# Attention logits with queries stacked as high over low part, and keys twice over each other

## The chip, the cores and the metric

The kernel runs on one core of one Trainium2 chip. The metric is the device time of one launch in microseconds. Engine names are short: PE is TensorE (matmul), ACT is ScalarE, DVE is VectorE, POOL is GpSimd, SP is SyncE, which here issues most DMA transfers. PSUM is the memory that PE writes its sums into, SBUF the one that holds everything else on the core.

## The reference

One decoder layer is computed on 256 tokens of 1024 features. The input is projected, three attention mixers share the projection, their outputs are gated, merged and normalised, and a feed-forward part follows:

```
proj = x @ w_in[i]
aq, ak, av, iq, ik, iw, bq, bk, bv, cq, ck, cv = jnp.split(proj, SPLIT_POINTS, axis=-1)
o_a = dsa_mixer(...)       # indexer scores pick 64 keys; 6 query heads on one shared key head
o_b = dilated_mixer(...)   # 3 groups x 4 query heads on 4 key heads
o_c = moba_mixer(...)      # 6 heads with a key head each
merged = sum of sigmoid(x @ w_gate) * (o @ w_br) over the three
x = layer_norm(ALPHA * x + merged @ w_out[i])
h = jnp.square(jax.nn.relu(x @ w_up[i])) @ w_down[i]
x = layer_norm(ALPHA * x + h + ple)
```

The part that matters here is the same in all mixers and in the indexer: for each head the logits, 64-long dot products of queries with keys,

```
logits = jnp.einsum('bqhd,bskd->bqhk', q, k) * HEAD_DIM ** -0.5     (then bias, mask, softmax)
```

There are 8 indexer heads, 12 dilated heads, 6 block heads and 6 sparse heads, 32 in all, over 256 queries in two blocks of 128.

## The kernel before, in words

All data is float32. PE multiplies in the faster float32r form, which keeps fewer bits, so every operand is split into a high part (the value cast to float32r) and a low part (what the cast lost). A product then takes three matmuls: high by high, high by low, low by high. `prod` (L127 to L129) does that for all large products. A split costs one ACT step, which casts, and one DVE step, which subtracts; for weights it is L70 (ACT) and L74 (DVE, and for part of the columns POOL).

The order of the work is as follows. The first four feature tiles (the indexer's queries) are projected with the arriving input (L402). Then one unit of weights after another is loaded by SP, split, and multiplied: `feat` projects 128 feature columns for all 256 tokens into one tile of the PSUM pool `mm`, and `fill` computes gates ("g") or merge products ("c") in between. `mm` has three tiles for all of these. Weights are split four units ahead. The code gives a priority by its order; a scheduler with a model of the time of each instruction draws up the order on each engine, and logits get a higher priority (L258).

A feature tile holds two heads of 64 features, head 0 on partitions 0 to 63 and head 1 on 64 to 127, as columns of tokens. `q_pair` (L204) splits such a tile of queries: one ACT step on all 128 partitions (L207) and one DVE step (L208). `k_pair` (L212) does it for keys (L218, L219). For the dilated and the block mixers it makes one ACT and one DVE step. For the two keys that all heads of a mixer share, `kI` (indexer) and `kA` (sparse mixer), it is called with the same 64 partitions twice and makes two of each, so that the key lies on both halves of the partitions.

`logits` (L254) takes a query tile and a key tile. For each of the two query blocks it makes six matmuls: low query by high key, high by high, high by low, each for head 1 and head 0. Each matmul uses 64 rows of the array, head 0 the upper and head 1 the lower, and `keep_in_program_order` (L267) keeps the two heads' matmuls side by side. The first query block needs 128 keys, the second 256. It is called 16 times: 4 for the indexer, 6 for the dilated mixer, 3 for the block mixer, 3 for the sparse one.

The logits then go through bias, softmax, transposes (L303 to L305) and the product with the values (L310 to L313); gates are read out of `mm` by ACT (L231), merge products by DVE (L244). After the mixers come the merge, the output projection, the normalisation and the feed-forward part.

Of the kernel before, what the change touches and what calls it, by code (L numbers as in the profile page):

```python
# [11 lines left out]
F32 = mybir.dt.float32  # L12
F32R = mybir.dt.float32r
ALU = mybir.AluOpType
# [6 lines left out]
S = 256  # L21
# [67 lines left out]
def hybrid_layer(ctx: ExitStack, tc: tile.TileContext, x0, xn, pT, wqk, wva, wvb, wg, wbc, wba,  # L89
                 wout, wup, wdn, wpg, wple, lnrow, rel, onehot, pick, out):  # L90
    nc = tc.nc
    pe, act, dve, pool = nc.tensor, nc.scalar, nc.vector, nc.gpsimd
# [48 lines left out]
    pm = mid.enter_context(tc.tile_pool(name="pm", bufs=1))  # L141
    one = ctx.enter_context(ExitStack())
    right = lambda n, b: one.enter_context(tc.tile_pool(name=n, bufs=b, side="right"))
    p1, k1, kp = (right(n, b) for n, b in (("p1", 1), ("k1", 2), ("kp", 3)))

    xh = p1.tile([128, KT, S], F32R, name="xh")
    xl = p1.tile([128, KT, S], F32R, name="xl")
# [12 lines left out]
    for t in TASKS:  # L160
# [4 lines left out]
        elif t in "gcao":  # L165
            u, w, n = {"g": (u_g, wg, 1024), "c": (u_bc, wbc, 640), "a": (u_ba, wba, 768),
                       "o": (u_out, wout, 1024)}[t]
# [28 lines left out]
    QC = (slice(0, 128), slice(128, 384))  # L196

    def mmbank(shape):
        t = mm.tile([128, 512], F32, name="mm", tag="mm")
        return t[:, 0:256] if shape == 256 else t  # L200

    last = [None]

    def q_pair(ps, scale=-0.125):  # L204

        q = qpool.tile([128, 2, S], F32R, name="q", tag="q")
        last[0] = act.mul(q[:, 0], ps, scale).ins  # L207
        dve.scalar_tensor_tensor(q[:, 1], ps, scale, q[:, 0].bitcast(F32), op0=ALU.mult,  # L208
                                 op1=ALU.subtract)
        return q  # L210

    def k_pair(a, b=None):  # L212


        k = (kp if b is None else k1).tile([128, 2, S], F32R, name="k", tag="k")
        for d, ps in ((slice(0, 128), a),) if b is None else ((slice(0, 64), a),
                                                             (slice(64, 128), b)):
            act.copy(k[d, 0], ps)  # L218
            dve.tensor_tensor(k[d, 1], ps, k[d, 0].bitcast(F32), op=ALU.subtract)  # L219
        return k  # L220

    n_g, n_c = [0], [0]

# [23 lines left out]
    def feat(f):  # L247
        ps = mmbank(256)
        gemm(ps, u_q[f], xs)
        if f > 4:  # L250
            next(side, None)
        return ps

    def logits(q, k):  # L254


        ss = [next(ps_s)[:, 0:384] for _ in range(2)]
        with tc.high_priority(offset=500):  # L258
            for b in range(2):
                c = slice(b * 128, (b + 1) * 128)  # L260
                for i, (x, y) in enumerate(((1, 0), (0, 0), (0, 1))):
                    for h in (1, 0):
                        d = slice(64 * h, 64 * h + 64)
                        m = pe.matmul(ss[h][:, QC[b]], lhsT=q[d, x, c],  # L264
                                      rhs=k[d, y, 0:128 * (b + 1)], start=i == 0, stop=i == 2)
                        if b or i or not h:
                            tc.keep_in_program_order(m)  # L267
        return ss

    V = p1.tile([128, 2, 11, 128], F32R, name="V")  # L270
# [71 lines left out]
    def slots(qs, k, Ts, vh, o):  # L342

        es = [wk2.tile([128, 3, 384], F32, name="eb", tag="eb") for _ in range(2)]
        mxs = [sm.tile([128, 2, 3], F32, name="mxb", tag="mxb") for _ in range(2)]
        for g in range(3):
            s = logits(qs[g], k)
            for h in range(2):
                for b, t in enumerate((Ts[h][:, g, 128:256], Ts[h][:, g, :])):
                    dve.tensor_tensor_reduce(es[h][:, g, QC[b]], s[h][:, QC[b]], t, op0=ALU.add,  # L350
                                             op1=ALU.min, scale=1.0, scalar=-GONE,
                                             accum_out=mxs[h][:, b, g:g + 1])
        for h in range(2):
            e = es[h]
            m = sm.tile([128, 2], F32, name="mx", tag="mx")
            den = sm.tile([128, 2], F32, name="den", tag="den")
            dve.tensor_reduce(m, mxs[h], axis=AX.X, op=ALU.min)
            for b in range(2):
                act.activation(e[:, :, QC[b]], e[:, :, QC[b]], AF.Exp, bias=m[:, b:b + 1],
                               scale=-1.0, accum_out=den[:, b:b + 1])  # L360
            pool.tensor_tensor(e[:, 0], e[:, 0], e[:, 1], op=ALU.add)
            pool.tensor_tensor(e[:, 0], e[:, 0], e[:, 2], op=ALU.add)
            scale_rows(e[:, 0], den)
            attend(e[:, 0], vh + h, o, h)
# [16 lines left out]
    with ExitStack() as begin:  # L381
        st = begin.enter_context(tc.tile_pool(name="st", bufs=1, side="right"))
        sh, sl = (st.tile([128, KT, FIRST * 128], F32R, name=n) for n in ("sh", "sl"))
        g0 = G.rearrange("p i s -> p (i s)").rearrange("p (k c) -> p k c", k=KT)
        cut = [((0, 384), (384, 768)) if k == 0 else ((0, 768),) for k in range(KT)]
        with tc.high_priority(offset=1000):
            for k in range(KT):
                for i, (a, b) in enumerate(cut[k]):
                    e = nc.scalar if i else nc.sync
                    e.dma_start(g0[:, k, a:b], x0[k, :, a:b])  # L390
            for k in range(KT):
                act.copy(xh[:, k], g0[:, k, 0:S])
                for a, b in cut[k]:
                    a = max(a, S)
                    act.copy(sh[:, k, a - S:b - S], g0[:, k, a:b])
                dve.tensor_tensor(xl[:, k], g0[:, k, 0:S], xh[:, k].bitcast(F32), op=ALU.subtract)
                dve.tensor_tensor(sl[:, k], g0[:, k, S:], sh[:, k].bitcast(F32), op=ALU.subtract)
        first = [next(ps_s if f < 3 else ps_t)[:, 0:S] for f in range(FIRST)]
        for k in range(KT):
            for i, (w, x) in enumerate(((sh, xh), (sh, xl), (sl, xh))):  # L400
                for f in range(FIRST):
                    pe.matmul(first[f], lhsT=w[:, k, 128 * f:128 * f + 128], rhs=x[:, k],  # L402
                              start=k == i == 0, stop=k == KT - 1 and i == 2)
        iq = [q_pair(ps, 0.125) for ps in first]
    tp, wk, wk2, sm = (right(n, b) for n, b in (("tp", 3), ("wk", 3), ("wk2", 2), ("sm", 6)))
    tab = bias_table()
    ps = feat(4)
    kI, kA = k_pair(ps[0:64], ps[0:64]), k_pair(ps[64:128], ps[64:128])

# [6 lines left out]
    for j in range(4):  # L418
        s = logits(iq[j], kI)
        r = wk2.tile([128, 768], F32, name="ri", tag="eb")  # L420
        r = r.rearrange("p (h k) -> p h k", h=2)
        for h in range(2):
            act.activation(r[:, h], s[h], AF.Relu)
            for b in range(2):
                n = 2 * j + h
                dve.scalar_tensor_tensor(idx[:, QC[b]], r[:, h, QC[b]], iw[:, b, n:n + 1],
                                         idx[:, QC[b]], op0=ALU.mult, op1=ALU.add)
# [16 lines left out]
    for j in range(2):  # L444
        ps = feat(5 + 4 * j)
        k = k_pair(ps)
        fill("g")
        qs = []
        for g in range(3):
            qs.append(q_pair(feat(6 + 4 * j + g)))  # L450
            if g:
                fill("g")
        o = opair()
        Ts = [toeplitz(6 + 2 * j + h, 4) for h in range(2)]
        slots(qs, k, Ts, 1 + 2 * j, o)
        pair_out(o, 3 + j)
        fill("g")
# [6 lines left out]
    for j in range(3):  # L464
        ps = feat(13 + 2 * j)
        k = k_pair(ps)
        q = q_pair(feat(14 + 2 * j))
        s = logits(q, k)
        o = opair()
        for h in range(2):  # L470
            n = 2 * j + h
            if n % 3 == 0:
                T = toeplitz(18 + n, 1)
            head(s, T[:, n % 3, 128:256], T[:, n % 3], 5 + n, o, h)
            fill("g")
        pair_out(o, 5 + j)
# [4 lines left out]
    for j in range(3):  # L481
        q = q_pair(feat(19 + j))
        s = logits(q, kA)
        o = opair()
        for h in range(2):
            n = 2 * j + h
# [144 lines left out]
    for b in range(2):  # L631
        t = slice(b * 128, (b + 1) * 128)
        for c in range(2):
            cs = slice(c * 512, (c + 1) * 512)
            ps = mmbank(512)
# [28 lines left out]
    for f in range(32):  # L664
        ps = mmbank(512).rearrange("p (b a t) -> p b a t", b=2, a=2)
# [4 lines left out]
        for k in range(KT):  # L670
            pe.matmul(ps[:, :, 0], lhsT=lo[:, cs[k]], rhs=x1[:, :, k, 0], start=False,  # L671
                      stop=k == KT - 1)
        r, q = (w2.tile([128, 2, 128], F32, name=n, tag=n) for n in ("r", "q2"))
# [3 lines left out]
        q = q.rearrange("p b t -> p (b t)")  # L677
# [126 lines left out]
```

## Time and profile before

| | |
|---|---|
| time, median of 3 runs | 452.64 us (451.95 to 453.76) |
| the profiled execution: time, span | 451.62 us, 449.8 us |
| instructions | 7880 |
| mean granted clock of TensorE | 0.996 |
| busy: PE, PE weight loads, DVE, ACT, POOL | 436.4, 396.1, 304.6, 260.9, 101.3 us |
| share of line 264 (logits) in the chain that ended last | 3.2% |

The span is the time from the first to the last instruction. The chain that ended last is followed back from the last instruction, at each step to what released it. Matmuls are pipelined: the time that a matmul lasts in a row is longer than the step from one to the next, so the start times of neighbours tell what one costs. In a row of the timeline the columns are the start (us), the duration (us), the engine, the line, the operation, output and inputs, the shape, and the number of instructions; the idle time before it and what ended it stand in brackets. In a group by line they are the output and inputs with shapes, the count, the busy us, the mean ns of one, and the idle us before with what ended it. In the waits they are the us in total, the times and the longest. In a stretch they are its bounds and length, and then the busy us and the count of PE, PEld (weight loads), DVE, ACT and POOL.

### The profile page before, as it was taken

How to read it: one execution, taken by the hardware profiler on the slowest of the kernel's cores; microseconds unless marked ns; L12 is line 12 of the kernel's file. 1: busy time of each engine (PE TensorE's matmuls, PEld its weight loads, DVE VectorE, ACT ScalarE, POOL GpSimd, SP SyncE). 2: the span in 40 equal slices, each digit the busy share in tenths (PEclk: the TensorE clock that was granted, in tenths of full speed). 3: DMA queues.
4: the chain of work that ended last, by engine and by line, in shares of the span. 5: the costliest groups of instructions: out<-in, count | busy, mean ns of one | idle time of the engine just before them, and what ended most of it. 6: DMA issues, size and time to landing. Idle time of an engine off the chain costs nothing.

```text
span 449.8 us, 7880 instructions
## 1 busy us (share of the span) xinstructions
PE 436.4 (97%) x2935; PEld 396.1 (88%) x2935; DVE 304.6 (68%) x561; ACT 260.9 (58%) x480; POOL 101.3 (23%) x99
## 2 busy tenths in 40 slices
PE   8999999998999999999999999999999999999993
PEld 8989999988999989999887888888888888888883
DVE  5878977456455677769958689888888644444555
ACT  6765465565787757757415468777777633333400
POOL 2744255478443545400001000000000000000000
PEclk9999999999999999999999999999999999999998
DMA  8883965539534345568952956665666566555202
GB/s 303 306 302 125 287 201 179 154 121 306 178 122 131 117 119 187 142 177 316 296 194 98 330 181 197 198 190 189 191 189 192 170 192 186 189 189 191 68 2 94
DMA packets 27147, 84.30 MB, mean 187 GB/s; under 512 B 2864, under 2 KB 6872, under 8 KB 26724
## 3 DMA queue, kind: packets, MB, share of 16 engines
q1 hardware_dynamic: 25872, 79.54, 54.9%
q10 hardware_dynamic: 1140, 4.19, 2.6%
q8 instruction: 23, 0.38, 0.4%
q14 instruction: 16, 0.13, 0.1%
q0 software_dynamic: 96, 0.06, 0.0%
HBM read 81.88 MB, written 1.90 MB: 186 GB/s over the span
## 4 chain that ended last, share of the span: by engine, by line
PE 87%; DVE 3%; DMA 3%; issue 3%; POOL 1%; ACT 1%; SPq 0%; POOLq 0%; DVEq 0%
PE mm L669 13%; PE mm L127 10%; PE mm L129 10%; PE mm L128 10%; PE b L129 9%; PE b L127 9%; PE b L128 9%; PE mm L671 7%; PE b L264 3%; PE b L402 3%; DMA relt<-in_pick_dram 1%; DMA T<-tabd 1%; DMA pr<-in_pT_dram 1%; DVE st L593 1%; PE b L123 1%
## 5 line engine op out<-in xcount | busy, mean ns | idle before, releaser
L74 DVE TENSOR_TENSOR wlo<-raw,whi 128x1024 fp32r<-128x1024 f32 (+5 forms) x138 | 148.8, 1084 | 72.6 <-ACT whi L70 69.0
L70 ACT CAST whi<-raw 128x1024 fp32r<-128x1024 f32 (+3 forms) x138 | 138.4, 1008 | 90.4 <-PE b L129 45.1
L127 PE MATMUL mm<-xh,whi 128*128 128x256 f32 x336 | 95.0, 283 | 1.0 <-DVE G L244 1.0
L74 POOL TENSOR_TENSOR wlo<-raw,whi 128x384 fp32r<-128x384 f32 (+3 forms) x58 | 77.0, 1334 | 84.2 <-ACT whi L70 76.6
L129 PE MATMUL mm<-xh,wlo 128*128 128x256 f32 x336 | 95.6, 284 | 0.0
L128 PE MATMUL mm<-xl,whi 128*128 128x256 f32 x336 | 94.7, 282 | 0.0
L127 PEld LDWEIGHTS mm<-xh,whi 128*128 128x128 f32 x336 | 63.4, 189 | 1.5 <-DVE G L244 1.2
L669 PE MATMUL mm<-x,whi 128*128 128x512 f32 x256 | 64.1, 392 | 0.0
L129 PEld LDWEIGHTS mm<-xh,wlo 128*128 128x128 f32 x336 | 63.3, 188 | 0.8
L128 PEld LDWEIGHTS mm<-xl,whi 128*128 128x128 f32 x336 | 63.3, 188 | 0.3
L600 POOL TENSOR_TENSOR rs<-rs,half 128x1 f32<-128x1 f32 x4 | 4.1, 1029 | 251.1 <-DVE rs L599 251.1
L669 PEld LDWEIGHTS mm<-x,whi 128*128 128x128 f32 x256 | 46.1, 189 | 8.3
L129 PE MATMUL b<-whi,hT 128*128 128x512 f32 (+1 forms) x150 | 52.6, 350 | 0.0
L128 PE MATMUL b<-wlo,hT 128*128 128x512 f32 (+1 forms) x150 | 52.2, 349 | 0.0
L127 PE MATMUL b<-whi,hT 128*128 128x512 f32 (+1 forms) x150 | 52.0, 348 | 0.0
L671 PEld LDWEIGHTS mm<-x,wlo 128*128 128x128 f32 x256 | 34.9, 190 | 2.5
L671 PE MATMUL mm<-x,wlo 128*128 128x256 f32 x256 | 35.7, 282 | 0.0
L127 PEld LDWEIGHTS b<-whi,hT 128*128 128x128 f32 x150 | 28.2, 188 | 4.1
L128 PEld LDWEIGHTS b<-wlo,hT 128*128 128x128 f32 x150 | 28.2, 188 | 4.1
L129 PEld LDWEIGHTS b<-whi,hT 128*128 128x128 f32 x150 | 28.2, 188 | 3.9
L674 DVE TENSOR_REDUCE r<-mm 128x256 f32<-128x512 f32 x32 | 22.1, 691 | 9.3 <-PE mm L671 9.3
L675 ACT ACTIVATE r<-r 128x256 f32<-128x256 f32 x32 | 13.4, 418 | 13.7 <-DVE r L674 13.7
(167 smaller groups left out, 701.4 us busy)
## 6 DMA issues: line engine op xcount, KB each, us to landing
raw<-in_wup_dram SPq DMA_DIRECT2D x32, 512.0 KB
raw<-in_wdn_dram SPq DMA_DIRECT2D x32, 512.0 KB
raw<-in_wg_dram SPq DMA_DIRECT2D x24, 512.0 KB
raw<-in_wqk_dram SPq DMA_DIRECT2D x18, 512.0 KB
raw<-in_wout_dram SPq DMA_DIRECT2D x8, 512.0 KB
raw<-in_wpg_dram SPq DMA_DIRECT2D x8, 512.0 KB
T<-tabd SPq DMA_DIRECT2D x24, 128.0 KB
G<-in_x_dram SPq DMA_DIRECT2D x7, 384.0 KB
```

The lines of the kernel that those rows point to most:

```text
L70: nc.scalar.copy(hi, r)
L74: e.tensor_tensor(lo[:, c], r[:, c], hi[:, c].bitcast(F32), op=ALU.subtract)
L123: pe.transpose(t[:, 0:128], ident, ident)
L127: pe.matmul(ps, lhsT=a[0], rhs=b[0], start=first, stop=False)
L128: pe.matmul(ps, lhsT=a[0], rhs=b[1], start=False, stop=False)
L129: pe.matmul(ps, lhsT=a[1], rhs=b[0], start=False, stop=last)
L264: m = pe.matmul(ss[h][:, QC[b]], lhsT=q[d, x, c], rhs=k[d, y, 0:128 * (b + 1)], start=i == 0, stop=i == 2)
L402: pe.matmul(first[f], lhsT=w[:, k, 128 * f:128 * f + 128], rhs=x[:, k], start=k == i == 0, stop=k == KT - 1 and i == 2)
L669: pe.matmul(ps, lhsT=hi[:, cs[k]], rhs=x1[:, :, k], start=k == 0, stop=False)
L671: pe.matmul(ps[:, :, 0], lhsT=lo[:, cs[k]], rhs=x1[:, :, k, 0], start=False, stop=k == KT - 1)
L674: dve.tensor_reduce(r, ps.rearrange("p b a t -> p b t a"), axis=AX.X, op=ALU.add)
L675: act.activation(r, r, AF.Relu)
```

## The change

Each head gets a query tile with 128 partitions: the high part on 0 to 63, the low part on 64 to 127. Its keys lie on both halves, with a high and a low part. One matmul over all 128 rows then sums high and low query times one key part, and two matmuls, with the key's high and low part, give the logits of a head and a query block. The product of the two low parts is now included.

`q_pair` therefore makes an ACT and a DVE step for each head, on 64 partitions; the DVE step reads partitions of the head and writes 64 to 127. `twice` puts a key on both halves, an ACT and a DVE step each; `k_pair` calls it for both heads of a tile and returns two tiles. `kI` and `kA` come from `twice` once each and are used for both heads. `logits` makes 8 matmuls of 128 rows instead of 12 of 64 rows, without the calls that keep their order. The pool `kp` gets 5 tiles instead of 3.

```
-    p1, k1, kp = (right(n, b) for n, b in (("p1", 1), ("k1", 2), ("kp", 3)))
+    p1, k1, kp = (right(n, b) for n, b in (("p1", 1), ("k1", 2), ("kp", 5)))
...
     def q_pair(ps, scale=-0.125):
         q = qpool.tile([128, 2, S], F32R, name="q", tag="q")
-        last[0] = act.mul(q[:, 0], ps, scale).ins
-        dve.scalar_tensor_tensor(q[:, 1], ps, scale, q[:, 0].bitcast(F32), op0=ALU.mult,
-                                 op1=ALU.subtract)
+        for h in range(2):
+            p = ps[64 * h:64 * h + 64]
+            last[0] = act.mul(q[0:64, h], p, scale).ins
+            dve.scalar_tensor_tensor(q[64:128, h], p, scale, q[0:64, h].bitcast(F32),
+                                     op0=ALU.mult, op1=ALU.subtract)
         return q
-    def k_pair(a, b=None):
-        k = (kp if b is None else k1).tile([128, 2, S], F32R, name="k", tag="k")
-        for d, ps in ((slice(0, 128), a),) if b is None else ((slice(0, 64), a),
-                                                             (slice(64, 128), b)):
+    def twice(pool, ps):
+        k = pool.tile([128, 2, S], F32R, name="k", tag="k")
+        for d in (slice(0, 64), slice(64, 128)):
             act.copy(k[d, 0], ps)
             dve.tensor_tensor(k[d, 1], ps, k[d, 0].bitcast(F32), op=ALU.subtract)
         return k
+    def k_pair(ps):
+        return [twice(kp, ps[64 * h:64 * h + 64]) for h in range(2)]
...
-                for i, (x, y) in enumerate(((1, 0), (0, 0), (0, 1))):
-                    for h in (1, 0):
-                        d = slice(64 * h, 64 * h + 64)
-                        m = pe.matmul(ss[h][:, QC[b]], lhsT=q[d, x, c],
-                                      rhs=k[d, y, 0:128 * (b + 1)], start=i == 0, stop=i == 2)
-                        if b or i or not h:
-                            tc.keep_in_program_order(m)
+                for h in range(2):
+                    for i in range(2):
+                        pe.matmul(ss[h][:, QC[b]], lhsT=q[:, h, c],
+                                  rhs=k[h][:, i, 0:128 * (b + 1)], start=i == 0, stop=i == 1)
...
-    kI, kA = k_pair(ps[0:64], ps[0:64]), k_pair(ps[64:128], ps[64:128])
+    kI, kA = [twice(k1, ps[0:64])] * 2, [twice(k1, ps[64:128])] * 2
```

## The prediction

> **What bounds the kernel now.** I read the page's first part, then the chain that ended last, then TensorE's own waits up to 211 us (the mixers end there), and then single stretches of the timeline.
>
> ```profile
> PE 436.4 (97%) x2935; PEld 396.1 (88%) x2935; DVE 304.6 (68%) x561; ACT 260.9 (58%) x480; POOL 101.3 (23%) x99
> PE 87%; DVE 3%; DMA 3%; issue 3%; POOL 1%; ACT 1%; SPq 0%; POOLq 0%; DVEq 0%
> ```
> ```profile
> PE b L303 <- POOL wlo L74: 1.2, 1, 1.2
> PE b L303 <- POOL eb L362: 1.0, 1, 1.0
> PE mm L127 <- DVE G L244: 1.0, 1, 1.0
> ```
> TensorE (PE) is busy 97% of the span and carries 87% of the chain. In the mixers its three longest waits make 3.2 us (1.2 + 1.0 + 1.0). So time taken from PE's instruction stream before 211 us comes off the end, and any new wait of PE there is added to it. VectorE (DVE) and ScalarE (ACT) count only where they make PE wait.
>
> **What the logits cost PE.** One of the 16 logits blocks, with its neighbours on PE:
>
> ```profile
> 71.28 0.28 PE L129 MATMUL mm<-xh,wlo 128*128 128x256 f32 x1
> ...
> 71.75 0.28 PE L127 MATMUL mm<-xh,whi 128*128 128x256 f32 x1
> 71.97 0.95 PE L264 MATMUL b<-k,q 64*128 64x128 f32 x12
> 72.85 0.39 PE L310 MATMUL b<-pth,V 128*128 128x256 f32 x1
> 73.07 0.28 PE L311 MATMUL b<-ptl,V 128*128 128x256 f32 x1
> ...
> 73.43 0.27 PE L303 MATMUL b<-ident,eb 128*128 128x128 f32 x1
> 73.54 0.27 PE L304 MATMUL b<-ident,eb 128*128 128x128 f32 x1
> ```
> Start times are what counts here, because the matmuls overlap. Four steps of 256 columns take 71.75 - 71.28 = 0.47 us, 0.1175 each. From the last matmul before the block to the second after it, 73.07 - 71.75 = 1.32 us pass. Two ordinary steps of 0.1175 lie in that, so the block costs 1.32 - 0.235 = 1.085 us. The step after a normal matmul is 0.22 at the way in and again at the way out (72.85 to 73.07), 0.1 more than usual each time, where the array changes between 64-row and 128-row use.
>
> The change puts 8 full-array matmuls in its place: 4 of 128 columns, 4 of 256. The step of a full-array matmul of 128 columns is 0.11 us by the two transposes (73.54 - 73.43); that is the only full-height 128-column pair near, so I take it. The new block is 4 x 0.11 + 4 x 0.1175 = 0.91 us. Gain: 0.175 us a block, **2.8 us over 16 blocks**. The bounds: if 128 columns went at half the 256-column step, the gain would be 1.085 - 4 x 0.059 - 4 x 0.1175 = 0.38 a block, 6.1 us; if they went at the full step, 1.085 - 0.94 = 0.145, 2.3 us. Fewer instructions (8 for 12) bring nothing beyond that.
>
> Here a rule speaks against the change. The Trainium skill (TensorE: Matmul & The Clock Gate, section Part 3: Packing small matmuls) says that matmuls on different row groups run concurrently, a pair costing little more than one. By it the old block would take six steps, 3 x 0.11 + 3 x 0.1175 = 0.68 us, and the change would lose 0.23 us a block, 3.7 us in all. The trace has 1.085 us instead, the change of use at both ends included, so the rule gets no chance of its own; the row is what the change removes.
>
> **What is added on ACT and DVE.** These are the costs of one step:
>
> ```profile
> L218 ACT CAST k<-mm 64x256 fp32r<-64x256 f32 x4 | 1.5, 365 | 1.3 <-DVE k L219 1.3
> L219 DVE TENSOR_TENSOR k<-mm,k 64x256 fp32r<-64x256 f32 x4 | 1.7, 420 | 0.1
> L208 DVE SCALAR_TENSOR_TENSOR q<-mm,q 128x256 fp32r<-128x256 f32 x12 | 5.0, 413 | 0.0
> 50.00:90.00 40.00, 40.00 (x345) 38.72 (x344) 27.34 (x101) 22.51 (x46) 19.32 (x17) 1.00 0.60 197
> ```
> Half the partitions cost the same: 365 ns on ACT and 420 ns on DVE at 64 x 256. Each of the 16 query pairs (12 from `mm`, 4 from the first bank tiles) goes from one ACT and one DVE step to two of each; each of the 5 key pairs of the dilated and block mixers goes from one of each to four of each. The two shared keys kI and kA keep their two of each. That is 16 + 15 = 31 more steps on each engine: 31 x 0.37 = 11.5 us of ACT, 31 x 0.42 = 13.0 us of DVE, spread over the mixers. As throughput this is covered: in the 40 us row DVE works 27.3 and ACT 22.5.
>
> **As a chain it is not covered.** The row of L218 shows ACT idle 1.3 us until DVE's L219. The shared keys at the start show how:
>
> ```profile
> 20.56 0.36 ACT L218 CAST k<-mm 64x256 fp32r<-64x256 f32 x1
> 23.23 0.36 ACT L218 CAST k<-mm 64x256 fp32r<-64x256 f32 x1 [0.67 <-DVE k L219]
> 24.90 0.37 ACT L218 CAST k<-mm 64x256 fp32r<-64x256 f32 x1 [0.23 <-DVE k L219]
> ```
> ```profile
> 22.79 0.41 DVE L219 TENSOR_TENSOR k<-mm,k 64x256 fp32r<-64x256 f32 x1
> 24.45 0.42 DVE L219 TENSOR_TENSOR k<-mm,k 64x256 fp32r<-64x256 f32 x1
> ...
> 27.67 0.43 DVE L219 TENSOR_TENSOR k<-mm,k 64x256 fp32r<-64x256 f32 x1
> ```
> ACT's second cast starts 0.03 us after DVE's first subtraction ends (22.79 + 0.41 = 23.20), and its third, which reads other partitions (64 to 127) and writes another tile, 0.03 us after the second (24.87). So ACT and DVE take turns on one `mm` tile, whatever part they read. Four such turns took 28.10 - 20.56 = 7.54 us; without any queueing they would take 4 x (0.365 + 0.42) + 7 x 0.03 = 3.35 us. The changed key pair is just such a chain of four turns on one tile, where one turn stood before; a query pair becomes two turns. While ACT stands at such a turn, the weight casts behind it in its queue stand too.
>
> The Trainium skill (PSUM — Partial Sum Buffer, section PSUM bank collisions raise a hardware error) says that two engines collide in a bank only within the same 32-partition quadrant, and that different quadrants may be used at once. By that rule the two heads of a pair could go side by side, two turns long. The 24.90 row, which waits across halves, shows that this program does not use it.
>
> **Who waits for the chain.** `mm` has three tiles, used in rotation:
>
> ```profile
> 162.03 0.39 PE L127 MATMUL mm<-xh,whi 128*128 128x256 f32 x1 [1.01 <-DVE G L244]
> ```
> ```profile
> 155.64 0.37 ACT L231 ACTIVATE G<-mm 128x256 f32<-128x256 f32 x1
> ```
> Before 162.03 PE stands 1.01 us for the tile that L244 still reads, although another tile had been read out at 156.0. So the third product after a key product must wait until that key's chain is over. The five key pairs, with the start of the ACT step, of the DVE step, and of the product that takes the tile next:
>
> ```profile
> 34.63 0.39 ACT L218 CAST k<-mm 128x256 fp32r<-128x256 f32 x1
> 65.29 0.36 ACT L218 CAST k<-mm 128x256 fp32r<-128x256 f32 x1
> 106.83 0.36 ACT L218 CAST k<-mm 128x256 fp32r<-128x256 f32 x1
> 118.95 0.35 ACT L218 CAST k<-mm 128x256 fp32r<-128x256 f32 x1
> 132.88 0.37 ACT L218 CAST k<-mm 128x256 fp32r<-128x256 f32 x1
> ```
> ```profile
> 35.92 0.41 DVE L219 TENSOR_TENSOR k<-mm,k 128x256 fp32r<-128x256 f32 x1
> 66.70 0.41 DVE L219 TENSOR_TENSOR k<-mm,k 128x256 fp32r<-128x256 f32 x1
> 107.76 0.42 DVE L219 TENSOR_TENSOR k<-mm,k 128x256 fp32r<-128x256 f32 x1
> 119.33 0.42 DVE L219 TENSOR_TENSOR k<-mm,k 128x256 fp32r<-128x256 f32 x1
> 133.63 0.42 DVE L219 TENSOR_TENSOR k<-mm,k 128x256 fp32r<-128x256 f32 x1
> ```
> ```profile
> 29.50 0.28 PE L127 MATMUL mm<-xh,whi 128*128 128x256 f32 x1
> 40.16 0.28 PE L127 MATMUL mm<-xh,whi 128*128 128x256 f32 x1
> 67.41 0.36 PE L127 MATMUL mm<-xh,whi 128*128 128x256 f32 x1
> 109.87 0.28 PE L127 MATMUL mm<-xh,whi 128*128 128x256 f32 x1
> 122.97 0.28 PE L127 MATMUL mm<-xh,whi 128*128 128x256 f32 x1
> 137.08 0.28 PE L127 MATMUL mm<-xh,whi 128*128 128x256 f32 x1
> ```
> Room from the ACT step to the reuse: 5.53, 2.12, 3.04, 4.02, 4.20 us. One turn took 1.70, 1.82, 1.35, 0.80, 1.17 us. Four turns at each pair's own length are 6.80, 7.28, 5.40, 3.20, 4.68 us, so PE would wait 1.27 + 5.16 + 2.36 + 0 + 0.48 = 9.3 us. The lower bound, 3.35 us everywhere, makes it 1.23 + 0.31 = 1.5 us; the upper, 7.54 us everywhere, 2.0 + 5.4 + 4.5 + 3.5 + 3.3 = 18.8 us. The second and third pair hold 7.5 of the 9.3 us, and both begin late, behind other ACT work. The order of all instructions is drawn up again for the changed kernel, and logits and attention products can fill part of a wait. I choose half of those two: 1.27 + 2.58 + 1.18 + 0.48 = **5.5 us**.
>
> Query pairs: one more turn is 0.8 us bare, 1.9 us at the pace of the shared keys (7.54 / 4). I take it to be covered at no cost by products already queued; uncovered it would delay a logits block by those amounts. The first four have a tighter place: kA's chain ends at 28.10 and the product at 29.50 takes its tile, 1.4 us of room. Four more DVE steps ahead of it are 4 x 0.42 = 1.7 us: **0.3 us** of waiting. The wider key pool (5 tiles, two a pair) costs nothing: its sixth tile returns to the first pair's, used long before.
>
> **Sum.** -2.8 + 5.5 + 0.3 = +3.0 us. The profiled execution took 451.62 us (span 449.8), which makes 454.6; it lies 1.02 us below the median of the runs, 452.64, so the forecast against that median is **455.6 us**. After 211 us nothing is touched and everything shifts along.
>
> **The rivals.** *PE's gain stays.* The reordered program starts the key chains early and puts other products in front of the tile's reuse; the waits stay under 0.5 us. Then 452.64 - 2.8 = 449.8 us. For it: 97% of PE is filled today, and three of five rooms exceed the bare chain. Against it: the room of 2.12 us is less than the bare 3.35. It decides from the point where all waits together are below 2.8 us, and shows beyond the measurement only below 0.5 us. *The two about cancel.* The halves of a key pair overlap so that a chain is two turns (3.40, 3.64, 2.70, 1.60, 2.34 us), and only the second exceeds its room, by 1.5 us: 452.64 - 2.8 + 1.5 + 0.3 = 451.6 us. The bare chain gives the same 1.5 us. For it is that these lengths are nearer to the bare cost; against it the 24.90 row. This is where the quadrant rule of the Trainium skill would lead. *Every chain takes the shared keys' 7.54 us:* 452.64 - 2.8 + 18.8 + 0.3 = 468.9 us. Against it: DVE is less loaded later than at the start. That the products do not become fewer I rule out: the shapes are written in the change.
>
> **How the numbers follow.** About 0.5%, 2.26 us, is what a measurement here can tell from no change. Forecast case 0.50 (its own range 452.5 to 460), gain stays 0.24, cancel 0.20, long chains 0.06. Slower by over 0.5% (above 454.9) takes 0.42 of the forecast case and the 0.06, so 0.48; within takes the rest of the forecast case and the cancelling one, 0.28; faster is 0.24. The range runs from just under the gain case, 449.3, to 461.5, which is near the own-length sum (452.64 - 2.8 + 9.3 + 0.3 = 459.4) with a little for queueing; it leaves out the long chains and a larger PE gain.
>
> **What would show it.** The new logits block should be 0.91 us with no 0.22 us steps around it. L218 and L219 should form groups of four alternating steps, ACT idle before each but the first until DVE's L219 or L208. PE should show waits at L127 for the key's DVE step, around the reuse of the key tiles. If those waits are missing, the forecast is wrong and the rival holds; if the block is not near 0.91 us, the PE term is.

## The result, and the profile after

The changed kernel took 455.46 us (median of 5 runs, 454.71 to 455.75). The kernel before took 451.95 us in the same series (5 runs, 451.42 to 453.76). The ratio is 1.0077, with a 95% interval of 1.006 to 1.0095: slower by 3.5 us. The forecast was 455.6 us. The profiled execution of the changed kernel took 455.75 us, with a span of 454.0 us, against 451.62 and 449.8 us before.

Busy time and the chain that ended last, from the page of the changed kernel:

```profile
PE 436.7 (96%) x2871; PEld 399.7 (88%) x2871; DVE 321.1 (71%) x592; ACT 273.9 (60%) x511; POOL 94.0 (21%) x99
PE 74%; DVE 3%; issue 2%; DMA 1%; POOL 1%; ACT 1%; POOLq 0%; DVEq 0%; ACTq 0%
```

PE has 64 matmuls fewer, ACT and DVE 31 steps more each, as counted. DVE gained 16.5 us and ACT 13.0 us of busy time, a little more than 13.0 and 11.5. One head of a logits block on PE:

```profile
61.98 0.28 PE L128 MATMUL mm<-xl,whi 128*128 128x256 f32 x1
62.10 0.62 PE L266 MATMUL b<-k,q 128*128 128x128 f32 x4
62.55 0.28 PE L129 MATMUL mm<-xh,wlo 128*128 128x256 f32 x1
62.67 0.28 PE L127 MATMUL mm<-xh,whi 128*128 128x256 f32 x1
```

Four matmuls take 62.55 - 62.10 = 0.45 us, so a block of two heads 0.90, where 0.91 was forecast and 1.085 stood before. The steps into it and out of it are 0.12 us, no longer 0.22. So far the change pays, about 16 x 0.18 = 2.9 us. It is lost again in waits. First PE's, up to 230 us (in us: total, times, longest), then those of ACT for the new steps:

```profile
PE b L266 <- DVE q L210: 4.4, 3, 2.4
PE b L123 <- POOL ident masks.py:199: 1.6, 1, 1.6
PE mm L127 <- ACT G L234: 1.0, 1, 1.0
PE b L310 <- ACT pth L306: 0.8, 1, 0.8
PE mm L127 <- DVE k L219: 0.6, 2, 0.4
PE b L374 <- DMA relt<-in_pick_dram: 0.4, 1, 0.4
PE mm L127 <- DVE q L210: 0.3, 1, 0.3
```
```profile
ACT q L209 <- DVE q L210: 10.5, 9, 3.6
ACT k L218 <- DVE k L219: 5.5, 5, 2.2
```

ACT stands 16 us in its queue for the turns, where it stood 1.3 us before. PE's three worst waits before (3.2 us) are gone from the list, and new ones stand there, the first of them at the logits. Of the 0.6 us for L219, the larger part lies at the two shared keys near the start; the two shorter waits for L210 lie further on:

```profile
29.84 0.35 PE L127 MATMUL mm<-xh,whi 128*128 128x256 f32 x1 [0.43 <-DVE k L219]
...
76.60 0.61 PE L266 MATMUL b<-k,q 128*128 128x128 f32 x3 [1.07 <-DVE q L210]
...
115.82 0.44 PE L266 MATMUL b<-k,q 128*128 128x128 f32 x2 [0.92 <-DVE q L210]
```

The longest wait, at 47.35, must be read with its neighbours on the three engines (PE, then DVE, then ACT):

```profile
41.85 0.39 PE L127 MATMUL mm<-xh,whi 128*128 128x256 f32 x1 [0.96 <-ACT G L234]
...
44.67 0.28 PE L129 MATMUL mm<-xh,wlo 128*128 128x256 f32 x1
47.35 0.72 PE L266 MATMUL b<-k,q 128*128 128x128 f32 x4 [2.40 <-DVE q L210]
48.22 0.36 PE L127 MATMUL mm<-xh,whi 128*128 128x256 f32 x1 [0.15 <-DVE k L219]
```
```profile
44.11 0.43 DVE L219 TENSOR_TENSOR k<-mm,k 64x256 fp32r<-64x256 f32 x1
...
46.87 0.42 DVE L210 SCALAR_TENSOR_TENSOR q<-mm,q 64x256 fp32r<-64x256 f32 x1
...
47.65 0.43 DVE L219 TENSOR_TENSOR k<-mm,k 64x256 fp32r<-64x256 f32 x1
```
```profile
36.65 0.37 ACT L218 CAST k<-mm 64x256 fp32r<-64x256 f32 x1
...
40.08 0.37 ACT L218 CAST k<-mm 64x256 fp32r<-64x256 f32 x1 [2.19 <-DVE k L219]
40.47 1.05 ACT L70 CAST whi<-raw 128x1024 fp32r<-128x1024 f32 x1
41.42 0.38 ACT L234 ACTIVATE G<-mm 128x256 f32<-128x256 f32 x1
41.82 0.37 ACT L218 CAST k<-mm 64x256 fp32r<-64x256 f32 x1
```

The profile names the query's step, since the logits are next in PE's queue. But the product behind them starts at 48.22, 0.14 us after the key's last subtraction ends (47.65 + 0.43 = 48.08): its tile of `mm` was held until then. Had the logits not stood in front, PE would have stood there nearly as long. The key chain itself began at 36.65 and had its fourth turn end at 48.08, 11.4 us, longer than the upper bound of 7.54. From the first L218 to the end of the last L219, the five key chains take 11.4, 9.9, 5.9, 8.0 and 5.8 us. The three waits for L210 at the logits lie inside such a chain, the first three of the five (36.65 to 48.08, 67.68 to 77.59, 111.71 to 117.59): the query steps stand between the turns of the keys. The gate at 41.42 shows the other side: ACT stood 2.19 us at a turn, the read-out of a gate and a weight cast were behind it, and PE waited 0.96 us for that tile. After the pause the clock drops. The stretch 35 to 52 us before, the same after, and the part at half clock (last columns: granted TensorE clock, DMA share, GB/s):

```profile
35.00:52.00 17.00, 17.00 (x157) 15.93 (x157) 14.76 (x49) 6.99 (x13) 7.21 (x5) 1.00 0.62 180
```
```profile
35.00:52.00 17.00, 13.49 (x101) 12.91 (x100) 16.66 (x48) 8.84 (x17) 4.76 (x4) 0.92 0.74 196
49.38:52.79 3.41, 3.41 (x19) 3.41 (x18) 3.29 (x12) 0.56 (x2) 0.00 (x0) 0.50 0.95 234
```

Half the clock over 3.41 us costs 1.7 us of full-speed time. With that the account nearly closes. The waits in the list make 7.5 us without the one at the very start, against 3.6 before (the three of 3.2 us and 0.4 for the bias table): 3.9 more. A pause also costs more than its listed wait: from 44.67 to 47.35 are 2.68 us, where an ordinary step is 0.12 and the wait is 2.40, so 0.16 more each, and 0.8 us for nine pauses instead of four. -2.9 + 3.9 + 0.8 + 1.7 = +3.5 us. The two profiled executions lie 4.1 us apart; 0.6 us of that is not placed.

### The profile page after: what moved, and what is told of

It reads as the page before. It is cut to its first block, busy times and chain, and to the rows that moved or that the text cites. A ratio compares the mean times of both kernels' runs of the same rounds, so it can differ in the third digit from the quotient of the medians.

```text
span 454.0 us, 7809 instructions
## 1 busy us (share of the span) xinstructions
PE 436.7 (96%) x2871; PEld 399.7 (88%) x2871; DVE 321.1 (71%) x592; ACT 273.9 (60%) x511; POOL 94.0 (21%) x99
## 4 chain that ended last, share of the span: by engine, by line
PE 74%; DVE 3%; issue 2%; DMA 1%; POOL 1%; ACT 1%; POOLq 0%; DVEq 0%; ACTq 0%
PE mm L669 13%; PE b L129 9%; PE b L127 9%; PE b L128 9%; PE mm L127 8%; PE mm L128 8%; PE mm L129 8%; PE mm L671 7%; PE b L266 2%; DMA raw<-in_wqk_dram 1%; DVE st L593 1%; DVE Y L610 1%; POOL wlo L74 0%; DVE Y L605 0%; PE b L311 0%
## 5 line engine op out<-in xcount | busy, mean ns | idle before, releaser
L74 DVE TENSOR_TENSOR wlo<-raw,whi 128x1024 fp32r<-128x1024 f32 (+5 forms) x138 | 152.1, 1109 | 60.9 <-ACT whi L70 57.9
L127 PE MATMUL mm<-xh,whi 128*128 128x256 f32 x336 | 95.8, 285 | 1.8 <-ACT G L234 1.0
L74 POOL TENSOR_TENSOR wlo<-raw,whi 128x384 fp32r<-128x384 f32 (+3 forms) x58 | 68.5, 1186 | 98.2 <-ACT whi L70 93.2
L127 PEld LDWEIGHTS mm<-xh,whi 128*128 128x128 f32 x336 | 63.9, 190 | 2.6 <-ACT G L234 1.2
L127 PE MATMUL b<-whi,hT 128*128 128x512 f32 (+1 forms) x150 | 52.0, 348 | 0.0
L127 PEld LDWEIGHTS b<-whi,hT 128*128 128x128 f32 x150 | 28.2, 188 | 4.1
L266 PE MATMUL b<-k,q 128*128 128x128 f32 (+1 forms) x128 | 20.0, 280 | 4.4 <-DVE q L210 4.4
```

The lines of the kernel that those rows point to most:

```text
L74: e.tensor_tensor(lo[:, c], r[:, c], hi[:, c].bitcast(F32), op=ALU.subtract)
L127: pe.matmul(ps, lhsT=a[0], rhs=b[0], start=first, stop=False)
L266: pe.matmul(ss[h][:, QC[b]], lhsT=q[:, h, c], rhs=k[h][:, i, 0:128 * (b + 1)], start=i == 0, stop=i == 1)
```

## The experiments

Each was timed in several rounds beside the kernel before, whose median was 452.12 us for e1 to e4, 451.92 for e5 to e8 and 451.78 for e9 to e12.

**e1: the matmuls alone.** In the kernel before, with its own query and key steps:

```
-                for i, (x, y) in enumerate(((1, 0), (0, 0), (0, 1))):
-                    for h in (1, 0):
...
+                for h in range(2):
+                    for i in range(2):
+                        pe.matmul(ss[h][:, QC[b]], lhsT=q[:, h, c],
+                                  rhs=k[:, i, 0:128 * (b + 1)], start=i == 0, stop=i == 1)
```

> The kernel before with the 8 full-array matmuls of 128 rows in place of the 12 of 64 rows, and its own steps for queries and keys (one ACT and one DVE step each). Which rows are summed changes: the two heads are mixed, so the logits are not the reference's; the work on PE is that of the changed kernel. Theory of the prediction (the matmul term is 16 x 0.17 us): 2.7 us faster than before, 0.6%, with the logits block at 0.92 us. Rival, that the new order of the program costs by itself: no faster, or slower, although no step was added on ACT and DVE.

Measured: 447.32 us, ratio 0.9895 (0.9882 to 0.9909), 4.8 us faster. That is 2 us more than the matmuls explain. PE's waits after 35 us are these:

```profile
PE b L308 <- DVE ptl L304: 0.3, 1, 0.3
PE b L307 <- ACT pth L303: 0.3, 1, 0.3
```

The logits are not the reference's, since the heads are mixed. The three waits of 3.2 us of the kernel before are not there. The program's order was drawn up anew, and what PE had waited for at the softmax's transposes (until 98.09 and 106.09 us) and for a merge product's tile (until 162.03) came in time. That fits the matmul term; that an edit also moves such waits by 2 to 3 us was not in the forecast.

**e2 and e3: the query steps alone, the key steps alone,** each on the kernel before with its 12 matmuls:

```
e2:
...
+        for d in (slice(0, 64), slice(64, 128)):
+            last[0] = act.mul(q[d, 0], ps[d], scale).ins
+            dve.scalar_tensor_tensor(q[d, 1], ps[d], scale, q[d, 0].bitcast(F32), op0=ALU.mult,
+                                     op1=ALU.subtract)
e3:
...
+            todo = ((k, lo, a[lo]), (k2, hi, a[lo]), (k2, lo, a[hi]), (k, hi, a[hi]))
+        for t, d, ps in todo:
+            act.copy(t[d, 0], ps)
+            dve.tensor_tensor(t[d, 1], ps, t[d, 0].bitcast(F32), op=ALU.subtract)
```

> The kernel before, its 12 matmuls kept, with each query pair split in two halves of 64 partitions: two ACT and two DVE steps in alternation, the data laid out as before. Theory A (the prediction's step: the query pairs are covered, only the key pairs cost): within 1 us of before. Theory B (from the trace of after, where PE waits 4.4 us in 3 places for the second DVE step of a query pair): 2 to 5 us slower, with PE waiting at the logits for the query's DVE step. Theory C (engine load: 13 us more DVE and 11.5 us more ACT work in all, half of it here): 1.5 to 2.5 us slower, as slow as the keys' part.

> The kernel before, its 12 matmuls and its query pairs kept, with each of the 5 key pairs made in four alternating turns of an ACT and a DVE step; the two turns that the old layout does not need write a second tile that nothing reads. Theory A (the prediction's step: the key chain holds its tile of the pool mm): 4 to 6 us slower, PE waiting at L127 for the key's DVE step. Theory B (what hurts is the query's second turn): within 1.5 us of before. Theory C (engine load): 1.5 to 2.5 us slower.

Measured: e2 455.25 us, ratio 1.0052 (1.0035 to 1.0069), 2.4 us by the ratio and 3.1 by the medians; its runs lie far apart, 453.58 to 459.31. e3 457.58 us, ratio 1.0119 (1.0103 to 1.0135), 5.5 us slower. The key steps cost as much as the forecast gave them, 5.5 us; the query steps, which it gave nothing, 2.4 us. The parts add up within their noise: -4.8 + 2.4 + 5.5 = +3.1, against +3.5 for the whole.

The traces do not show the expected paths, though. In e3 no wait of PE names the key's step (there L223). The longest for a tile of `mm` is for a query's step:

```profile
PE mm L127 <- DVE q L208: 1.8, 2, 1.1
```

Its two places, 73.48 and 115.33 us, lie inside the second and third key chain (65.66 to 75.84, 110.89 to 116.64). That the key chain pushed the query back is likely but not shown: ACT had stood 1.27 us for a softmax step of POOL before 69.60. Part of e3's cost is the clock. It was halved from 73.30 to 76.71 us in the profiled execution, which took 457.93 us; two of its four runs show a mean clock of 0.996 and took 456.57 and 457.43. The trace of e2 is that of the execution of 459.31 us, with two stretches of 3.41 us at half clock; PE waits there 0.6 us for the query's step. So e2 fits theory B and theory C alike.

**e4: casts first.** The changed kernel, its steps in another order:

```
-        for h in range(2):
-            p = ps[64 * h:64 * h + 64]
-            last[0] = act.mul(q[0:64, h], p, scale).ins
-            dve.scalar_tensor_tensor(q[64:128, h], p, ...)
+        for h in range(2):
+            last[0] = act.mul(q[0:64, h], ps[64 * h:64 * h + 64], scale).ins
+        for h in range(2):
+            dve.scalar_tensor_tensor(q[64:128, h], ps[64 * h:64 * h + 64], ...)
```

and in the same way for the four casts and four subtractions of a key pair.

> The changed kernel, all its steps kept, in another order: for a query pair both ACT casts and then both DVE subtractions, for a key pair the four casts and then the four subtractions, and the same for the two shared keys in one chain. The two engines then change place on a tile once instead of three times (query) or seven times (key). Theory A and B (the chain of turns is the cost): ACT's waits for L210 and L219 go from 16 us to under 3, and the time is 2 to 5 us below the changed kernel, 450.5 to 453.5 where before is 452. Theory C (engine load, the number of steps): no different from the changed kernel, 455.5.

Measured: 454.92 us, ratio 1.0059 (1.0043 to 1.0075); the changed kernel had 1.0077. ACT's waits for the turns are gone, and so, in the profiled execution, are PE's for the query step and the drop of the clock (1.00 in each of the stretches from 17 to 211 us). The five key chains are together less than half as long, 4.4, 3.3, 3.3, 4.0 and 3.3 us. PE now waits elsewhere:

```profile
PE b L304 <- POOL wlo L74: 2.7, 2, 1.4
PE b L123 <- POOL ident masks.py:199: 1.6, 1, 1.6
PE mm L127 <- DVE k L220: 1.2, 3, 0.4
PE b L304 <- POOL eb L362: 1.0, 1, 1.0
PE mm L127 <- DVE G L248: 1.0, 1, 1.0
```

Apart from the second row, which is the start, these are mostly the waits of the kernel before, at the softmax's transposes and a merge product's tile: 4.7 us where those were 3.2. With the turns away, what is late next is the softmax. So the turns are not the whole cost; of the 2 to 5 us expected from taking them away, less than 1 came, and the intervals of e4 and the changed kernel overlap.

**e5, e6, e7: spare steps.** e1 plus steps that nobody waits for, on both engines, on DVE, on ACT:

```
+    def spare(n):
+        for _ in range(n):
+            act.copy(da, xh[0:64, 0].bitcast(F32))
+            dve.tensor_tensor(dd, xh[0:64, 0].bitcast(F32), xl[0:64, 0].bitcast(F32),
+                              op=ALU.subtract)
```

> The kernel of e1 (8 full-array matmuls, the steps of before, heads mixed) plus 31 spare steps on ACT and 31 on DVE of 64 x 256 elements, one pair of them after each query pair and three after each of the 5 key pairs. They read the input in SBUF and write a tile that nothing reads: no tile of mm, no turn, nobody waits for them. e1 took 447.3 us and e4, with as many real steps and one change of engine on each tile, 454.9. Load theory (the steps cost as time in the queues of ACT and DVE, whoever reads them): 452 to 455 us. Chain theory (they cost because the query, the key and the tile wait for them): below 449 us.

> The kernel of e1 plus the 31 spare steps on DVE alone. Load theory, if DVE is the engine that is short (85% busy from 17 to 50 us in the kernel before): nearly all of what e5 loses, 451 to 454 us. Chain theory: below 449 us.

> The kernel of e1 plus the 31 spare steps on ACT alone. Load theory with DVE short: below 449 us, that is within 1.5 us of e1. If ACT is short: 451 to 454 us. Chain theory: below 449 us.

Measured: 453.55, 453.17 and 448.68 us (ratios 1.0041, 1.0028, 0.9929): 6.2, 5.9 and 1.4 us above e1. By the medians that is the load theory with DVE short. The traces show where the time went. PE's waits in e6 from 17 to 211 us:

```profile
PE b L382 <- DMA relt<-in_pick_dram: 2.1, 1, 2.1
PE mm L127 <- DVE k L228: 2.1, 1, 2.1
PE b L319 <- DVE ptl L315: 0.4, 1, 0.4
PE b L318 <- ACT pth L314: 0.3, 1, 0.3
PE b L318 <- DVE o L324: 0.3, 1, 0.3
```

The first two are over at 35 us. The spare steps were ready at once and went to the front: all 31 of e6 start between 4.7 and 44.4 us, 24 of them before 35 us (the row has the count, the shortest, median and longest in ns, the first and last start, and the shape):

```profile
L209 DVE TENSOR_TENSOR dd<-xh,xl x31: 406/414/1231, 4.7 to 44.4; 64x256 f32<-64x256 f32 x31
```

The first wait came by way of POOL, whose first four splits took longer than in e1 (first e1, then e6):

```profile
15.10 4.71 POOL L74 TENSOR_TENSOR wlo<-raw,whi 128x384 fp32r<-128x384 f32 x4 [12.14 <-ACT whi L70]
19.76 0.73 POOL L367 DMA_DIRECT2D oh<-in_onehot_dram  x1
```
```profile
14.50 7.44 POOL L74 TENSOR_TENSOR wlo<-raw,whi 128x384 fp32r<-128x384 f32 x4 [11.54 <-ACT whi L70]
21.88 0.73 POOL L378 DMA_DIRECT2D oh<-in_onehot_dram  x1
```

The bias table's loads, next in POOL's queue, went out 2.1 us later (21.88 for 19.76), and PE stood there. The second wait is load on DVE: the spare steps stood between the subtractions of the two shared keys, whose chain took 10.4 us instead of 7.1 in e1, and PE waited for their tile (DVE, then PE):

```profile
33.90 0.43 DVE L228 TENSOR_TENSOR k<-mm,k 64x256 fp32r<-64x256 f32 x1
```
```profile
34.47 0.36 PE L127 MATMUL mm<-xh,whi 128*128 128x256 f32 x1 [2.09 <-DVE k L228]
```

Then the clock was halved from 34.98 to 38.40 us, 1.7 us. 2.1 + 2.1 + 1.7 = 5.9 us is the whole distance from e1. Later PE waits 1.0 us in all (0.4 + 0.3 + 0.3), where e1 has 0.6, but only seven spare steps start after 35 us and none after 44.4. So at the start added DVE steps did cost, in front of a chain that PE waited for. e5 shows the same way, with 3.0 us for the bias table and 6.83 us at half clock. e7 stays below 449 us, as the chain theory and the load theory with DVE short both have it. On load in the later stretch, where the five key pairs and most query pairs lie, these experiments say next to nothing, and the expectation of e9 below, which takes such load to be free, rests on those seven steps.

**e8: zero keys.** Another layout with few added steps:

```
+        for h, ps in enumerate((a[0:64], a[64:128]) if b is None else (a, b)):
+            d = slice(64 * h, 64 * h + 64)
+            act.copy(k[d, 0, h], ps)
+            dve.tensor_tensor(k[d, 1, h], ps, k[d, 0, h].bitcast(F32), op=ALU.subtract)
...
+                    pe.matmul(ss[b], lhsT=q[:, x, c], rhs=k[:, y, :, 0:128 * (b + 1)],
+                              start=i == 0, stop=i == 2)
```

> Full-array matmuls with few added steps: the query tile stays as before (head 0 on the upper, head 1 on the lower 64 partitions, one ACT and one DVE step), and the keys stand in tiles with zeros in the other head's half, head 0 and head 1 beside each other, so that one matmul gives both heads: 3 matmuls of 256 and 3 of 512 columns a block, 3 x 0.117 + 3 x 0.23 = 1.04 us, 0.7 us less than before over 16 blocks. A key pair takes two ACT and two DVE steps, 5 more of each in all instead of 31. If the steps are what costs (7.6 us for 31 from e1 to e4, so 1.2 us for 5) and the other 2 us of e1's gain come with every block that keeps the array in one use: 449.5 to 451.5 us, below before by about 1.5. If only the PE term counts: 452.5.

Measured: 452.63 us, ratio 1.0019 (1.0008 to 1.0031). That is the 452.5 of the matmul term alone, not the 449.5 to 451.5 with e1's extra gain, so that gain did not come with full-array use as such. The wait for a merge product's tile is there again, and one at the attention product is new:

```profile
PE b L312 <- DVE o L318: 1.5, 1, 1.5
PE mm L127 <- DVE G L250: 1.0, 1, 1.0
```

**e9 to e12: first in the queue.** e9 puts the steps of the changed kernel at the priority of the logits, e10 those of the kernel before, e11 those of e4; e12 is e11 with the key's second half copied by ACT:

```
e9, e10, e11:
...
+        with tc.high_priority(offset=500):
e12:
...
+            for k, d, o in zip(ks, two, two[::-1]):
+                act.copy(k[o], k[d].bitcast(F32))
```

> The changed kernel, with the ACT and DVE steps of the query and key pairs drawn up at the higher priority that the logits already have (+500); number, alternation and operands of the steps are the same. e5 and e6 lost their time at the start, where spare steps between SBUF operands slowed POOL; after 35 us their spare DVE steps cost nothing, so load alone is not it. Queue theory (the chains are long because each turn waits behind weight splits and top-k steps): PE's 4.4 us of waits for L210 fall below 1, the granted clock no longer drops, 451 to 453 us. Turn theory (the alternation itself): no better than 455. Order theory (any new order of the program moves the stalls by some us): anything between 450 and 457, with the stalls at other places.

> Control: the kernel before with the same higher priority on its own query and key steps. Queue theory: those chains were short and covered, so within 1 us of before (451 to 453). Order theory: it moves by as much as e9 does against the changed kernel.

> e4 (casts first, one change of engine on a tile) with the higher priority on the query and key steps: both the alternation and the queueing are gone. Queue theory: the shortest chains of all kernels with the full steps, 449 to 451.5 us, faster than before by up to 0.6%. If it stays at e4's 455, the steps cost by something that neither chain nor queue explains.

> e11 with the second half of each key tile copied by ACT from the first half in SBUF: a key pair is two ACT casts, two DVE subtractions, after which the tile of mm is free, and two ACT copies of 64 x 512; 12 DVE steps fewer than in e11. Queue theory: the tile is released earlier, 448.5 to 451 us. If DVE time as such counts: faster than e11 by 12 x 0.42 = 5 us at most.

Measured: e9 454.85 us (1.0072, 1.0054 to 1.009), e10 451.64 (1.0000, 0.9988 to 1.0012), e11 453.19 (1.0039, 1.0024 to 1.0053), e12 453.47 (1.0038, 1.0024 to 1.0051). e9 has the changed kernel's wait again, at the same place and of the same length:

```profile
44.41 0.28 PE L129 MATMUL mm<-xh,wlo 128*128 128x256 f32 x1
47.08 0.68 PE L268 MATMUL b<-k,q 128*128 128x128 f32 x3 [2.39 <-DVE q L211]
```

But e9 is no test of the queue theory. Its trace has the same instructions in the same order on PE, ACT, DVE and POOL as that of the changed kernel, and e10 that of the kernel before but for one ACT step moved by one place: the higher priority left the order as it was, so e9 and e10 repeat those two kernels. The queue theory stays untested there. In e11 the order did change. Its five key chains take 4.4, 3.3, 3.3, 3.3 and 3.3 us, close to the bare 4 x (0.365 + 0.42) = 3.1, so neither alternation nor queueing is left in most of them. It lies 0.38% below the changed kernel (1.0039 to 1.0077), 1.7 us, and misses the expected 449 to 451.5. Part of the 1.7 us is the clock: seven of its twelve runs show a mean clock of 0.994 to 0.996 and took 451.98 to 453.27 us, five show 0.991 or 0.992 and took 454.02 to 454.90; all five runs of the changed kernel lie at 0.990 to 0.993. No profile of one of those five runs of e11 exists. e12, with 12 DVE steps fewer than e11, is no faster and misses its 448.5 to 451. Of the kernels that compute the whole layer none was faster than the kernel before.

## Why the prediction was right in its number, point by point

*The matmul term: right.* 0.90 us a block for a forecast of 0.91, no longer steps at the ends, 2.9 us for 2.8. The rule of the Trainium skill that row groups run side by side (TensorE: Matmul & The Clock Gate, section Part 3: Packing small matmuls) did not price the change, as the block's own row had said.

*The counts: right.* 31 steps on each engine, half the partitions at the same duration. The change of turns on one tile is in the trace: ACT waits 10.5 + 5.5 us for it, and in e4 those waits are gone. The quadrant rule of the Trainium skill (PSUM — Partial Sum Buffer, section PSUM bank collisions raise a hardware error) is not used by the changed program either: in the query pairs too ACT's cast of one half waits for DVE's step on the other.

*"The third product after a key product must wait until that key's chain is over": wrong as put.* The tiles did not rotate there. The product at 41.85 took the gate's tile while the key's chain ran on until 48.08. That made the waits at the key tiles themselves small: of the 0.6 us that the profile names for L219, 0.43 is at the shared keys, where the forecast had 0.3, and 0.15 at the five key pairs, where it had 5.5. Even with the 2.4 us at 47.35, where the key's tile was held as well, it is less than half. The chains were longer than the forecast's own-length estimates, 11.4, 9.9, 5.9, 8.0 and 5.8 us, where 6.8, 7.3, 5.4, 3.2 and 4.7 were taken. The one error lowered the waits, the other raised them. The forecast had named these waits at L127 as its own sign, and by that sign its main term is not borne out; the rival that PE's gain stays did not hold either.

*"Query pairs: covered at no cost": wrong.* e2 shows 2.4 us. In the changed kernel PE's waits for the query's step are 4.4 us, its largest entry. All three lie inside a key chain, and at the longest a key's tile, held to 48.08, would have kept PE as long, so keys and queries cannot be divided by the profile's names there. e3 gives the keys 5.5 us in the kernel before, a drop of the clock in some of its runs included.

*What was not in the forecast:* the clock's drop, 1.7 us by the granted clock, and that a newly drawn order can take 2 to 3 us of waits at the softmax and the merge away (e1).

*The sum.* Forecast: -2.8 + 5.8 = +3.0. Measured by parts: -4.8 (e1, with 2 us of vanished waits) + 5.5 + 2.4 = +3.1, the whole +3.5. In place of the 5.8 us of waits at L127, the trace of the changed kernel has 3.9 us more of waits, nearly all at other places, 0.8 us for the greater number of pauses and 1.7 us of clock. That the added steps cost more than the matmuls gain is shown by e1, e2 and e3. That they cost as a chain and not as throughput is shown only for a small part. The steps cost 3.5 + 2.9 = 6.4 us in the changed kernel; in e11, with chains of nearly bare length, they still cost 1.8 + 2.9 = 4.7. So shorter chains, and with them a steadier clock, are worth about 1.7 us there. That the total came out to 0.2 us is largely luck: the main term stood at the wrong place, the query's cost, the clock and the gain of e1 were missing, and these errors happened to cancel.

*What stays open.* Why e11 is still 6.5 us above e1 by the ratios (1.0039 to 0.9895, 1.44% of 452). Apart from the start, its longest waits are at the softmax's transposes and the merge product's tile, as in the kernel before, and e1's order avoids them:

```profile
PE b L306 <- POOL wlo L74: 1.4, 1, 1.4
PE mm L127 <- DVE G L250: 1.0, 1, 1.0
```

What in the scheduler's plan decides that was not tried. Nor was load on ACT and DVE after 45 us. A full DVE alone does not stop PE everywhere: in e1, from 35 to 52 us, DVE was busy all 17 us, and so was PE.

```profile
35.00:52.00 17.00, 17.00 (x147) 17.00 (x146) 17.00 (x61) 7.72 (x13) 5.26 (x5) 1.00 0.71 206
```

## What to carry to other kernels

Added steps on an engine with room can still cost: here 31 on each of two engines took back more than the 2.9 us that the matmuls gained. When two engines take turns on one PSUM tile, count the turns until the tile is free, not only the busy time. Letting one engine do all its reads before the other starts halved these chains (e4), but was worth under 1 us by itself and 1.7 us with the higher priority (e11). When the program's order is drawn up again by a scheduler, expect other waits to come or go by as much as a small change is worth, and test the parts of the change separately. Before reading the time of such a test, see in its trace that the edit did what it was made for: here a higher priority left the order as it was (e9), and spare steps meant for the whole kernel all ran in its first 45 us (e6).

## What the runs showed of the hardware beside that

A pause of PE of 2.4 us, with 0.96 us of waiting shortly before, was followed by 3.41 us at half the granted clock, and every other stretch of half clock between 10 and 440 us in these traces also goes with waits of PE shortly before or at its start: 2.39 us in e9, 0.95 and 1.05 us in e3, 0.86 and 0.61 us and later 2.29 us in e2, 2.09 us in e6, and 3.01 us in e5, there with 6.83 us at half clock. The length of one wait does not decide it: a wait of 2.11 us in e6 (until 28.64 us) had no drop behind it for 6 us, and one of 1.42 us in e4 none at all. And added DVE steps with both operands in SBUF, set beside POOL's splits, went with POOL taking 7.44 us (e6) and 7.20 us (e5) instead of 4.71 (e1, and e7 with spare steps on ACT alone) for the same four.
